# Inner RMS norms of a macaron layer: 1/rms spread over the partitions by fp32r hi/lo matmuls, the third norm summed over features by the same matmuls

## The chip, the cores and the metric

One core of one Trainium2 chip runs the whole layer in one launch. The metric is the device time of that launch in microseconds; lower is better. The kernel before takes 864.71 us, the median of three runs (863.97 to 865.85).

## What is computed

One encoder layer on x of 512 tokens by 1024 features, all in float32:

```
x = x + 0.5 * swiglu(rms(x, g1), gate1, up1, down1)      # 1024 -> 2816 -> 1024
x = x + mixer(rms(x, g2))                                # attention heads and a pooling mixer
x = x + 0.5 * swiglu(rms(x, g3), gate2, up2, down2)
x = rms(x, g4)
rms(x, g) = x * rsqrt(mean(x * x over the 1024 features) + 1e-6) * g
```

The three inner norms (the first three `rms`) are the subject here. Each token needs one number, 1/rms, and every product that follows has to be multiplied by it at some point.

## The kernel before

x lies transposed in SBUF: eight tiles of 128 features by 512 tokens. A product in float32 is made of fp32r operands: each operand is split into a rounded part `hi` (a cast on ScalarE, ACT below) and the rest `lo` (a subtraction on VectorE, DVE below), and `mm3` (lines 176 to 178) issues three matmuls of TensorE (PE below), hi*hi, hi*lo and lo*hi, into one PSUM bank. A weight panel of 128x1024 is fetched into a `raw` tile (SP's DMA queue, line 169), cast to `whi` and reduced to `wlo` (lines 131 and 132), and then feeds 24 matmuls of 512 columns. The `hi` and `lo` panels have three buffers in one pool and one in another, so a panel's cast waits until PE is through with the panel four before it.

`Norm` holds one inner norm. `add` (lines 134, 135) splits x times the gain into the token operands `hhi`, `hlo`, without 1/rms, since a factor per token can be put in after the product. `square` (lines 283 to 287) adds up x*x over the eight feature tiles in `acc`, 128 by 512. `per_token` then sums `acc` over the partitions: four fp32 matmuls, each with a 128x128 block of `acc` stationary and one column of ones moving (line 291), give one number per token in a 128x4 layout. ACT takes the root (line 298), DVE makes 1/rms of it with one Newton step on four columns (lines 301 and 261 to 264) and multiplies it into the identity (line 304), which gives `diag`, four diagonal 128x128 blocks side by side. `spread` multiplies a matrix of ones by `diag` in one fp32 matmul of 512 columns (line 312; the trace shows it as two records) and ACT copies the bank to `rb` (line 314): 1/rms of every token, the same in all 128 partitions.

`rb` has two kinds of readers, all on DVE: eight `aside` tiles x * gain * rb (line 337), from which later Strassen-like blocks of the up projection are built (lines 343, 131 to 135), and the evacuation of the gate banks (lines 395 and 399, with SiLU on ACT at 397 and the product with `up` at 687).

Each FFN begins with four banks, `first`, that take the first two feature blocks of gate and up; four panels feed them. `norm.finish()` (which calls `per_token` and `spread`) stands ahead of the last of these panels, at high priority: the Tile scheduler puts its instructions as early as their inputs allow. In the first FFN the tiles of x arrive by DMA one after the other, so this falls into the last panel of `first`. In the second FFN all of x is there, and it falls into the first panel. There it stands beside eight transposed copies of x (PE line 1431, ACT line 1435, a DMA to `x_d` at line 1436), which save x for the end. After `first`, blocks 2 to 4 are made one after the other in banks that are reused in turn: the third panel pair's first bank is `first[0]`'s, so PE cannot begin it before DVE has read `first[0]` (line 395).

The second norm sits in the mixer stage, whose order is written by a planner: generators record the instructions of PE, ACT, DVE and POOL in the order of an estimated clock. `finish_norm` there calls `per_token` and `spread` when the third weight panel is in use; its costs in the planner are not touched by the change. This norm uses `r`, the 128x4 form, as well: the projections to q, k and v put tokens on partitions.

The queues work in order: PE, ACT and DVE each take their instructions as they stand, and one that waits holds all behind it.

Of the kernel before, what the change touches and what calls it, by code (L numbers as in the profile page):

```python
# [16 lines left out]
P = 128  # L17
D = 1024
S = 512
KD = D // P  # L20
NT = S // P
# [7 lines left out]
EPS = 1e-6  # L29
# [24 lines left out]
def layer(  # L54
# [31 lines left out]
    nc = tc.nc  # L86

    const = ctx.enter_context(tc.tile_pool(name="const", bufs=1))
# [4 lines left out]
    small = ctx.enter_context(tc.tile_pool(name="small", bufs=2))  # L93
# [7 lines left out]
    def name(what):  # L101
        n_tiles[0] += 1
        return f"{what}_{n_tiles[0]}"

    def temp(dtype=F32):
        return tpool.tile([P, S], dtype, tag="t", name=name("t"))

    def bank(tag="mm", bufs=4):
        return ps.tile([P, S], F32, tag=tag, name=name(tag), bufs=bufs)

    def abank():
        return bank("a", 4)
# [15 lines left out]
    def split(src, hi, lo, scale=None):  # L128

        if scale is None:  # L130
            nc.scalar.copy(hi, src)  # L131
            nc.vector.tensor_tensor(lo, src, hi.bitcast(F32), op=ALU.subtract)  # L132
        else:
            nc.scalar.activation(hi, src, AF.Copy, scale=scale)
            nc.vector.scalar_tensor_tensor(
                lo, src, scale, hi.bitcast(F32), op0=ALU.mult, op1=ALU.subtract
            )
# [25 lines left out]
    def weights(src, parts=1):  # L163
        n = src.shape[-1]
        raw = raw_tile()
        hi, lo = part_tiles()
        for i in range(parts):
            part = slice(i * n // parts, (i + 1) * n // parts)
            nc.sync.dma_start(raw[:, part], src[:, part])
            split(raw[:, part], hi[:, part], lo[:, part])  # L170
        return hi, lo

    def mm3(acc, a, b, start, stop, further=False):

        more = dict(skip_group_check=True) if further else {}
        nc.tensor.matmul(acc, a[0], b[0], start=start, stop=False, **more)  # L176
        nc.tensor.matmul(acc, a[0], b[1], start=False, stop=False, **more)  # L177
        nc.tensor.matmul(acc, a[1], b[0], start=False, stop=stop, **more)  # L178

    def cut(pair, lo, n):  # L180
        if isinstance(pair[0], list):
            pair, lo = [z[lo // S] for z in pair], lo % S
        return pair[0][:, lo : lo + n], pair[1][:, lo : lo + n]
# [11 lines left out]
    ident = const.tile([P, P], F32, name="ident")  # L195
    make_identity(nc, ident)
    ones = const.tile([P, P], F32, name="ones")
    table = const.tile([P, 2], F32, name="table")
    nc.vector.memset(ones, 1.0)
    eps = table[:, 1:2]  # L200
    nc.vector.memset(eps, EPS)

    def tables(func, after):

        nc.scalar.activation(table[:, 0:1], after, func, scale=0.0)
# [49 lines left out]
    def rsqrt_of(v, root, out):  # L255

        n = v.shape[-1]
        y, a, b = (
            small.tile([P, n], F32, tag=f"rs{n}", name=name("rs"), bufs=3) for _ in range(3)
        )  # L260
        nc.vector.reciprocal(y, root)
        nc.vector.tensor_tensor(a, y, y, op=ALU.mult)
        nc.vector.scalar_tensor_tensor(b, a, -0.5, v, op0=ALU.mult, op1=ALU.mult)
        nc.vector.scalar_tensor_tensor(out, b, 1.5, y, op0=ALU.add, op1=ALU.mult)

    class Norm:
# [22 lines left out]
        def per_token(self, total, after=None):  # L289
            for t in range(NT):  # L290
                nc.tensor.matmul(
                    total[:, t : t + 1], self.acc[:, t * P : (t + 1) * P], ones[:, 0:1],
                    start=True, stop=True,
                )
            v, root, self.r = (
                small.tile([P, NT], F32, tag=what, name=name(what)) for what in ("v", "root", "r")
            )
            nc.scalar.activation(root, total[:, :NT], AF.Sqrt, scale=1.0 / D, bias=eps)
            if after:
                tables(after, root[:, 0:1])  # L300
            nc.vector.tensor_scalar(v, total[:, :NT], 1.0 / D, EPS, op0=ALU.mult, op1=ALU.add)
            rsqrt_of(v, root, self.r)
            self.diag = temp()
            nc.vector.tensor_tensor(
                self.diag.rearrange("p (t c) -> p t c", t=NT),
                ident.unsqueeze(1).to_broadcast([P, NT, P]),
                self.r.unsqueeze(2).to_broadcast([P, NT, P]),
                op=ALU.mult,
            )

        def spread(self, wide):
            nc.tensor.matmul(wide, ones, self.diag, start=True, stop=True)
            self.rb = small.tile([P, S], F32, tag="rb", name=name("rb"), bufs=1)
            nc.scalar.copy(self.rb, wide)

        def finish(self):
            self.per_token(abank(), AF.Silu)
            self.spread(abank())

        def blocks(self, pool, aside):  # L320

# [61 lines left out]
    def ffn_up(norm, wA, down, loaded):  # L383
# [22 lines left out]
        for kp in range(KD // 2):  # L406
            if not loaded:
                load(2 * kp)
            w = weights(wA[kp], 1 if loaded or kp else 4)
            if not loaded:  # L410
                load(2 * kp + 1)
                norm.square(2 * kp)
                norm.square(2 * kp + 1)
            if kp == KD // 2 - 1:
                with tc.high_priority():
                    norm.finish()
            for kk in range(2):
                k = 2 * kp + kk
                for j in range(4):
                    mm3(first[j], cut(w, (kk * 4 + j) * P, P), norm.h[k], k == 0, k == KD - 1)  # L420
# [127 lines left out]
        with tc.manual_schedule(engines={E.PE, E.DVE, E.Activation, E.SP}):  # L548
            last_silu = last_place = last_sums = nothing
            for n in range(PLAIN, KF):  # L550
                f = down.order[n]
                acc, up_lo, up_hi = bank()[:, :HT], bank()[:, :HT], abank()[:, :HT]
                u, z, sg = temp(), temp(), temp()
# [228 lines left out]
    def load(k):  # L782
        nc.sync.dma_start(x[k], xT[k])
        n1.add(k, square=False)
# [19 lines left out]
    with tc.tile_pool(name="act1", bufs=1, reuse_waits="tile") as apool:  # L804
        down1.begin(apool)
        ffn_up(n1, wA1, down1, loaded=False)
        p1, p5, p6 = whole(bank), whole(bank), whole(abank)

# [9 lines left out]
        with tc.manual_schedule(engines={mybir.EngineType.SP}):  # L818
# [3 lines left out]
            y = [down1.acts[i // 2][:, i % 2].rearrange("p k c -> p (k c)") for i in range(2 * NT)]  # L822
# [42 lines left out]
    with tc.tile_pool(name="mix", bufs=1, reuse_waits="tile") as mpool:  # L865
# [146 lines left out]
        v, done, scored, turned = [None] * NT, {}, set(), set()  # L1012
# [392 lines left out]
        bias = [None] * NH  # L1405
# [18 lines left out]
    with tc.tile_pool(name="act2", bufs=1, reuse_waits="tile") as apool:  # L1424
        down2.begin(apool)

        for half in range(2):
            for t in range(NT):
# [5 lines left out]
                z = temp()  # L1434
                nc.scalar.copy(z, tp)
                nc.sync.dma_start(x_d[half * NT + t], z)
        ffn_up(n3, wA2, down2, loaded=True)
        xt = [hpool.tile([P, S], F32, tag="h", name=name("xt")) for _ in range(2 * NT)]
        rooms.extend((xpool, f"x{i}", 1, 2 * S) for i in range(KD // 2))
# [28 lines left out]
        def mean(t, parts):  # L1468

            v = eps  # L1470
            for part in parts:
                u = column("u")
                nc.vector.scalar_tensor_tensor(
                    u, ssq[:, t, part : part + 1], 1.0 / D, v, op0=ALU.mult, op1=ALU.add
                )
                v = u
            return v
# [79 lines left out]
        with tc.manual_schedule(engines={E.PE, E.DVE, E.Activation}):  # L1557
            for tt in range(2):
                t = 2 + tt
                for i, at in enumerate(p7[tt]):  # L1560
                    for g, a, w in late:
                        down2.mms([[at]] * 2, g, a, w, (tt,), further=True)
                    residual(0, t, *at, scale=-0.5)
                    if i == 0 and tt:
                        settle(0, t, 0, *at[1:])
                        finish(t - 1, mean(t - 1, [1]), 0)
                        v = mean(t, [1, 0])
                    else:
                        settle(0, t, 2 * i, *at[1:])
            finish(t, v, 2)  # L1570
# [81 lines left out]
```

## Time and profile before

| what | us |
|---|---|
| median of three runs | 864.71 (863.97 to 865.85) |
| profiled execution, its own time | 865.0 |
| its span in the trace | 863.2 |
| PE busy | 848.8 |
| DVE busy | 708.3 |
| ACT busy | 501.1 |
| mean granted TensorE clock | 0.998 |

The span is what the trace covers from the first to the last instruction; the profiled execution's own time is 1.8 us longer. Both stand beside the median without a correction: 865.0 is 0.3 above 864.71. Start times in all lines are microseconds from the start of the span. In a timeline a row has start, duration, engine, line, operation and tiles, with the idle time ahead of it and what ended that in square brackets. Matmuls overlap: a matmul of 512 columns is shown with about 0.39 us but the next one starts some 0.23 us later. What a matmul costs in a full queue is the distance from start to start.

### The profile page before, as it was taken

How to read it: one execution, taken by the hardware profiler on the slowest of the kernel's cores; microseconds unless marked ns; L12 is line 12 of the kernel's file. 1: busy time of each engine (PE TensorE's matmuls, PEld its weight loads, DVE VectorE, ACT ScalarE, POOL GpSimd, SP SyncE). 2: the span in 40 equal slices, each digit the busy share in tenths (PEclk: the TensorE clock that was granted, in tenths of full speed). 3: DMA queues.
4: the chain of work that ended last, by engine and by line, in shares of the span. 5: the costliest groups of instructions: out<-in, count | busy, mean ns of one | idle time of the engine just before them, and what ended most of it. 6: DMA issues, size and time to landing. Idle time of an engine off the chain costs nothing.

```text
span 863.2 us, 14110 instructions
## 1 busy us (share of the span) xinstructions
PE 848.8 (98%) x5296; PEld 757.5 (88%) x5296; DVE 708.3 (82%) x1115; ACT 501.1 (58%) x859; POOL 120.1 (14%) x196
## 2 busy tenths in 40 slices
PE   9999999999999999989999999999999999999996
PEld 7889999999988888867878788889999999988885
DVE  7999898898897769685878667969888898887896
ACT  7445555555676556548647756445555555566573
POOL 0124322222000000120011000102112111122000
PEclk9999999999999999999999999999999999999999
DMA  8199998877576764322212026248778778899832
GB/s 291 57 285 248 293 277 207 202 206 165 144 242 204 254 212 136 97 86 85 75 57 90 25 73 244 80 140 228 212 231 202 189 199 209 251 328 341 274 109 98
DMA packets 72244, 158.50 MB, mean 184 GB/s; under 512 B 6112, under 2 KB 29168, under 8 KB 71792
## 3 DMA queue, kind: packets, MB, share of 16 engines
q1 hardware_dynamic: 49088, 110.93, 36.8%
q0 software_dynamic: 22656, 46.14, 24.7%
q8 instruction: 41, 0.67, 0.3%
q10 hardware_dynamic: 432, 0.54, 0.2%
q14 instruction: 27, 0.22, 0.1%
HBM read 153.38 MB, written 50.34 MB: 236 GB/s over the span
## 4 chain that ended last, share of the span: by engine, by line
PE 91%; DVE 3%; DMA 2%; ACT 2%; issue 1%; SPq 0%; ACTq 0%; DVEq 0%
PE mm L176 22%; PE mm L177 21%; PE mm L178 21%; PE a L176 7%; PE a L177 7%; PE a L178 7%; DMA raw<-in_wA_dram 2%; PE a L1172 1%; PE a L1226 1%; PE a L1214 1%; DVE t L1093 1%; DVE wlo L449 1%; ACT prob L1153 1%; PE a L211 0%; PE a L1431 0%
## 5 line engine op out<-in xcount | busy, mean ns | idle before, releaser
L132 DVE TENSOR_TENSOR wlo<-raw,whi 128x1024 fp32r<-128x1024 f32 (+2 forms) x115 | 125.0, 1096 | 20.7 <-ACT whi L131 20.4
L131 ACT CAST whi<-raw 128x1024 fp32r<-128x1024 f32 (+2 forms) x115 | 106.9, 944 | 57.7 <-PE mm L177 15.5
L177 PE MATMUL mm<-ha,whi 128*128 128x256 f32 x408 | 115.6, 283 | 0.0
L178 PE MATMUL mm<-ha,wlo 128*128 128x256 f32 x408 | 115.0, 282 | 0.0
L176 PE MATMUL mm<-ha,whi 128*128 128x256 f32 x408 | 115.0, 282 | 0.0
L540 ACT ACTIVATE t<-mm 128x256 f32<-128x256 f32 x102 | 39.2, 384 | 121.5 <-PE mm L178 120.8
L449 DVE TENSOR_TENSOR wlo<-wsum,whi 128x1024 fp32r<-128x1024 f32 x68 | 83.0, 1220 | 14.1 <-ACT whi L444 14.1
L178 PEld LDWEIGHTS mm<-ha,wlo 128*128 128x128 f32 x408 | 77.4, 190 | 0.0
L176 PEld LDWEIGHTS mm<-ha,whi 128*128 128x128 f32 x408 | 77.2, 189 | 0.1
L177 PEld LDWEIGHTS mm<-ha,whi 128*128 128x128 f32 x408 | 77.2, 189 | 0.1
L176 PE MATMUL mm<-hhi,whi 128*128 128x512 f32 x192 | 76.0, 399 | 0.0
L177 PE MATMUL mm<-hlo,whi 128*128 128x512 f32 x192 | 75.7, 395 | 0.0
L178 PE MATMUL mm<-hhi,wlo 128*128 128x512 f32 x192 | 74.8, 392 | 0.0
L677 POOL DMA_DIRECT2D wsum<-in_wB_dram x72 | 70.4, 1147 | 11.7 <-issue 8.5
L444 ACT CAST whi<-wsum 128x1024 fp32r<-128x1024 f32 x68 | 67.9, 1048 | 4.1 <-PE mm L177 3.9
L177 PE MATMUL mm<-wlo,ah 128*128 128x512 f32 x176 | 68.6, 390 | 0.0
L178 PE MATMUL mm<-whi,ah 128*128 128x512 f32 x176 | 68.5, 389 | 0.0
L176 PE MATMUL mm<-whi,ah 128*128 128x512 f32 x176 | 68.4, 390 | 0.0
L675 POOL COPY mark<-t 128x1 f32<-128x1 f32 x40 | 15.1, 377 | 382.1 <-DVE t L585 228.0
L449 DVE TENSOR_TENSOR wlo<-raw,whi 128x512 fp32r<-128x512 f32 x68 | 62.5, 951 | 3.4 <-ACT whi L444 3.4
L444 ACT CAST whi<-raw 128x512 fp32r<-128x512 f32 x68 | 56.3, 828 | 11.4 <-DMA raw<-in_wA_dram 6.9
L132 DVE TENSOR_TENSOR ah<-acts,ah 128x512 fp32r<-128x512 f32 (+1 forms) x72 | 45.7, 641 | 14.5 <-ACT ah L131 14.2
(211 smaller groups left out, 2381.5 us busy)
## 6 DMA issues: line engine op xcount, KB each, us to landing
raw<-in_wA_dram SPq DMA_DIRECT2D x87, 512.0 KB, 5.5
wsum<-in_wB_dram POOLq DMA_DIRECT2D x60, 512.0 KB, 7.7
raw<-wsum SPq DMA_DIRECT2D x40, 512.0 KB, 4.4
raw<-in_wB_dram SPq DMA_DIRECT2D x30, 512.0 KB, 4.7
wsum<-wsum POOLq DMA_DIRECT2D x20, 512.0 KB, 5.8
x<-in_xT_dram SPq DMA_DIRECT2D x16, 256.0 KB, 5.7
raw<-in_wQK_dram SPq DMA_DIRECT2D x8, 512.0 KB, 3.5
raw<-in_wO_dram SPq DMA_DIRECT2D x8, 512.0 KB, 3.4
```

What stands on the lines that cost most here:

```text
L131: nc.scalar.copy(hi, src)
L132: nc.vector.tensor_tensor(lo, src, hi.bitcast(F32), op=ALU.subtract)
L176: nc.tensor.matmul(acc, a[0], b[0], start=start, stop=False, **more)
L177: nc.tensor.matmul(acc, a[0], b[1], start=False, stop=False, **more)
L178: nc.tensor.matmul(acc, a[1], b[0], start=False, stop=stop, **more)
L444: nc.scalar.copy(hi, src)
L449: nc.vector.tensor_tensor(lo, src, hi.bitcast(F32), op=ALU.subtract)
L540: nc.scalar.activation(dst, src, AF.Copy, scale=scale)
L675: nc.gpsimd.tensor_copy(mark, after[:, 0:1])
L677: nc.gpsimd.dma_start(self.rows(i, g), self.rows(self.terms[i][at], g), **(dict(accum_op=ALU.add) if at else {}),)
L1093: nc.vector.tensor_tensor(q3, q3, rs[:, t, :].unsqueeze(2).to_broadcast([P, 8, HD]), op=ALU.mult)
L1153: nc.scalar.activation(p, p, AF.Copy, scale=rt)
```

## The change

All three norms: 1/rms is split into `r_hi` (fp32r) and `r_lo` on four columns, two diagonals of fp32r are made, and `spread` is two fp32r matmuls with a matrix of ones in fp32r (`ones_r`, a new tile that is cast once at the start).

The third norm (`after` is None): `acc` itself is split into a fp32r pair, and the two matmuls with `ones_r` sum it over the features and put the sum into all 128 partitions at once. There is no 128x4 form any more: root, reciprocal and Newton step run on 512 columns, and the last of these instructions writes `rb`.

```diff
+    ones_r = const.tile([P, P], F32R, name="ones_r")
     nc.vector.memset(ones, 1.0)
+    nc.vector.tensor_copy(ones_r, ones)
...
             rsqrt_of(v, root, self.r)
-            self.diag = temp()
-            nc.vector.tensor_tensor(diag, ident, self.r, op=ALU.mult)
+            r_hi = small.tile([P, NT], F32R, tag="r_hi", name=name("r_hi"))
+            r_lo = small.tile([P, NT], F32, tag="r_lo", name=name("r_lo"))
+            nc.vector.tensor_copy(r_hi, self.r)
+            nc.vector.tensor_tensor(r_lo, self.r, r_hi.bitcast(F32), op=ALU.subtract)
+            self.diag = [temp(F32R), temp(F32R)]
+            for z, r in zip(self.diag, (r_hi.bitcast(F32), r_lo)):
+                nc.vector.tensor_tensor(z, ident, r, op=ALU.mult)
+        def over_rows(self, wide, pair):
+            for i, z in enumerate(pair):
+                nc.tensor.matmul(wide, ones_r, z, start=i == 0, stop=i == 1)
         def spread(self, wide):
-            nc.tensor.matmul(wide, ones, self.diag, start=True, stop=True)
-            self.rb = small.tile([P, S], F32, tag="rb", name=name("rb"), bufs=1)
+            self.over_rows(wide, self.diag)
+            self.rb = self.broadcast()
             nc.scalar.copy(self.rb, wide)
-        def finish(self):
-            self.per_token(abank(), AF.Silu)
-            self.spread(abank())
+        def finish(self, after=None):
+            if after is not None:
+                self.per_token(abank(), after)
+                self.spread(abank())
+                return
+            pair, total = (temp(F32R), temp(F32R)), abank()
+            split(self.acc, *pair)
+            self.over_rows(total, pair)
+            root, v, y = temp(), temp(), temp()
+            nc.scalar.activation(root, total, AF.Sqrt, scale=1.0 / D, bias=eps)
+            tables(AF.Silu, root[:, 0:1])
+            nc.vector.tensor_scalar(v, total, 1.0 / D, EPS, op0=ALU.mult, op1=ALU.add)
+            nc.vector.reciprocal(y, root)
+            nc.vector.tensor_tensor(root, y, y, op=ALU.mult)
+            nc.vector.scalar_tensor_tensor(v, root, -0.5, v, op0=ALU.mult, op1=ALU.mult)
+            self.rb = self.broadcast()
+            nc.vector.scalar_tensor_tensor(self.rb, v, 1.5, y, op0=ALU.add, op1=ALU.mult)
...
-                    norm.finish()
+                    norm.finish(None if loaded else AF.Silu)
```

(The views of `diag` and of its operands are written short here.) Line numbers behind the change are larger: 291 becomes 293, 304 becomes 311, 312 becomes 320, 337 becomes 366, 395 becomes 424, 1435 becomes 1464; tile numbers differ as well.

Where the instructions stand. First norm, PE, in the last panel of `first`. Before, the one fp32 matmul with the diagonal `t_353`:

```order
L176 MATMUL mm_166<-hhi_314,whi_319 128x512
L312 MATMUL a_355<-t_353,ones 128x512
L177 MATMUL mm_166<-hlo_315,whi_319 128x512
L178 MATMUL mm_166<-hhi_314,wlo_320 128x512
L176 MATMUL mm_163<-hhi_325,whi_319 128x512
```

Of the change, the same place; `t_359` and `t_360` are the two diagonals:

```order
L177 MATMUL mm_168<-hlo_317,whi_321 128x512
L320 MATMUL a_363<-t_359,ones_r 128x512
L178 MATMUL mm_168<-hhi_316,wlo_322 128x512
L176 MATMUL mm_165<-hhi_327,whi_321 128x512
L320 MATMUL a_363<-t_360,ones_r 128x512
L177 MATMUL mm_165<-hlo_328,whi_321 128x512
```

The first of the two stands one matmul later than the old one, the second four matmuls later.

On DVE the first norm's rows of the change behind 1/rms (`r_344`) are these, in place of one row L304:

```order
L307 CAST r_hi_355<-r_344 128x4
L308 TENSOR_TENSOR r_lo_356<-r_344,r_hi_355 128x4
L311 TENSOR_TENSOR t_359<-ident,r_hi_355 128x512
L311 TENSOR_TENSOR t_360<-ident,r_lo_356 128x512
L132 TENSOR_TENSOR wlo_517<-raw_515,whi_516 128x1024
```

Before, one `aside` (L337) stood between that `wlo` and the first evacuation (L395); now the evacuation comes straight behind the `wlo`.

Third norm, PE, in the first panel of the second FFN. `a_5962` and `a_5978` are the last of the eight transposed blocks. Before:

```order
L1431 MATMUL a_5962<-ident,x_3046 128x128
L291 MATMUL a_6070<-ones,acc_5763 128x1 x4
L1431 MATMUL a_5962<-ident,x_3046 128x128
L176 MATMUL mm_5972<-hhi_5759,whi_5975 128x512
L177 MATMUL mm_5972<-hlo_5760,whi_5975 128x512
```

Of the change, from the last transposes to the first matmul with `ones_r`:

```order
L1460 MATMUL a_5978<-ident,x_3055 128x128 x2
L176 MATMUL mm_5988<-hhi_5775,whi_5991 128x512
L177 MATMUL mm_5988<-hlo_5776,whi_5991 128x512
L178 MATMUL mm_5988<-hhi_5775,wlo_5992 128x512
L176 MATMUL mm_5989<-hhi_5775,whi_5991 128x512
L177 MATMUL mm_5989<-hlo_5776,whi_5991 128x512
L178 MATMUL mm_5989<-hhi_5775,wlo_5992 128x512
L176 MATMUL mm_5986<-hhi_5795,whi_5991 128x512
L177 MATMUL mm_5986<-hlo_5796,whi_5991 128x512
L320 MATMUL a_6088<-t_6086,ones_r 128x512
```

The four matmuls with `acc` are gone. The first L320 stands eight matmuls behind the transposes, the second (of `t_6087`, the rest of `acc`) two more matmuls of the panel later; before, L312 stood thirteen matmuls behind the transposes.

ACT at the same place, of the change, from the last copy of x on. `t_6086` is the fp32r part of `acc`, the root is `t_6093`:

```order
L1464 COPY t_5983<-a_5978 128x512
L131 CAST t_6086<-acc_5779 128x512
L131 CAST whi_6021<-raw_6020 128x1024
L131 CAST whi_6051<-raw_6050 128x1024
L340 ACTIVATE t_6093<-a_6088,table 128x512
L131 CAST whi_6081<-raw_6080 128x1024
L207 ACT_TABLE_LOAD
L207 ACTIVATE table<-t_6093 128x1
L131 CAST whi_6146<-raw_6145 128x1024
L131 CAST whi_6181<-raw_6180 128x1024
```

Before, the root of four columns and the table load stood between the sixth and the eighth copy, ahead of all weight casts; now all eight copies come first, and two weight casts stand ahead of the root.

DVE at the same place, of the change, from the split of `acc` to the first evacuation:

```order
L132 TENSOR_TENSOR t_6087<-acc_5779,t_6086 128x512
L132 TENSOR_TENSOR wlo_6022<-raw_6020,whi_6021 128x1024
L132 TENSOR_TENSOR wlo_6052<-raw_6050,whi_6051 128x1024
L342 TENSOR_SCALAR t_6094<-a_6088 128x512
L343 RECIPROCAL t_6095<-t_6093 128x512
L132 TENSOR_TENSOR wlo_6082<-raw_6080,whi_6081 128x1024
L344 TENSOR_TENSOR t_6093<-t_6095 128x512
L132 TENSOR_TENSOR wlo_6147<-raw_6145,whi_6146 128x1024
L345 SCALAR_TENSOR_TENSOR t_6094<-t_6093,t_6094 128x512
L132 TENSOR_TENSOR wlo_6182<-raw_6180,whi_6181 128x1024
L347 SCALAR_TENSOR_TENSOR rb_6102<-t_6094,t_6095 128x512
```

Behind these stand the eight `aside` rows (L366) and then the first evacuation (L424). Before, six small rows (L301 to L304) came first, and the eight `aside` rows stood between the `wlo` rows; three wide rows on `aside` (L343) that stood ahead of the first evacuation now stand behind it. The second norm (mixer) has two L320 rows in the place of L312 and the same two added DVE rows as the first.

More of the change, by code (lines that the diff above doesn't have):

```diff
@@ L302, in per_token @@
             rsqrt_of(v, root, self.r)
-            self.diag = temp()
[L304 to L309, printed above, removed]
+            r_hi = small.tile([P, NT], F32R, tag="r_hi", name=name("r_hi"))
+            r_lo = small.tile([P, NT], F32, tag="r_lo", name=name("r_lo"))
+            nc.vector.tensor_copy(r_hi, self.r)
@@ new lines, in per_token @@
+            nc.vector.tensor_tensor(r_lo, self.r, r_hi.bitcast(F32), op=ALU.subtract)
+            self.diag = [temp(F32R), temp(F32R)]
+            for z, r in zip(self.diag, (r_hi.bitcast(F32), r_lo)):
+                nc.vector.tensor_tensor(
+                    z.rearrange("p (t c) -> p t c", t=NT),
+                    ident.unsqueeze(1).to_broadcast([P, NT, P]),
+                    r.unsqueeze(2).to_broadcast([P, NT, P]),
+                    op=ALU.mult,
+                )
+        def over_rows(self, wide, pair):
+            for i, z in enumerate(pair):
+                nc.tensor.matmul(wide, ones_r, z, start=i == 0, stop=i == 1)
@@ L311, in spread, with broadcast @@
+        def broadcast(self):
+            return small.tile([P, S], F32, tag="rb", name=name("rb"), bufs=1)
         def spread(self, wide):
-            nc.tensor.matmul(wide, ones, self.diag, start=True, stop=True)
-            self.rb = small.tile([P, S], F32, tag="rb", name=name("rb"), bufs=1)
+            self.over_rows(wide, self.diag)
+            self.rb = self.broadcast()
             nc.scalar.copy(self.rb, wide)
-        def finish(self):
-            self.per_token(abank(), AF.Silu)
-            self.spread(abank())
+        def finish(self, after=None):
[15 more added lines that the diff above has]
+            nc.vector.scalar_tensor_tensor(self.rb, v, 1.5, y, op0=ALU.add, op1=ALU.mult)
```

## The prediction, made before the changed kernel was run

> **What bounds the kernel now.** First the shares of the chain of waits, from the page: which engine, followed back from the last instruction, set the end.
>
> ```profile
> PE 91%; DVE 3%; DMA 2%; ACT 2%; issue 1%; SPq 0%; ACTq 0%; DVEq 0%
> ```
>
> TensorE sets it. Then the busy time of the engines in four stretches (columns: PE, PEld, DVE, ACT, POOL, clock, DMA share, GB/s): the first FFN's first Strassen blocks, the mixer, the second FFN's start, its down projection.
>
> ```profile
> 50.00:110.00 60.00, 58.94 (x445) 56.39 (x444) 53.52 (x76) 32.46 (x57) 20.36 (x26) 1.00 1.03 276
> 370.00:515.00 145.00, 140.59 (x725) 111.79 (x724) 108.57 (x258) 92.60 (x193) 14.89 (x21) 1.00 0.19 68
> 532.00:560.00 28.00, 28.00 (x125) 23.18 (x125) 27.93 (x35) 11.06 (x13) 3.26 (x3) 1.00 0.37 131
> 620.00:760.00 140.00, 140.00 (x1139) 138.20 (x1138) 121.76 (x171) 81.42 (x144) 24.76 (x42) 1.00 0.79 218
> ```
>
> PE does not pause behind the third norm (532 to 760), at full clock, so a pass less there ends the kernel earlier; but DVE is full from 532 to 560 as well, so work moved to DVE there needs care. The first stretch has full DMA queues, the second a few PE gaps. Last the chain in order of time, at the norms:
>
> ```profile
> 25.85 0.86 PE a L312 x2
> ...
> 75.86 10.56 DMA raw<-in_wA_dram
> ...
> 96.74 10.18 DMA raw<-in_wA_dram
> ...
> 360.24 0.86 PE a L312 x2
> ...
> 525.03 0.90 PE a L291 x8
> ...
> 528.86 0.23 PE mm L176
> 529.09 0.86 PE a L312 x2
> ```
>
> All three spreads and the third norm's sum are on the chain: 0.86 us each for the fp32 matmul of 512 columns, 0.90 us for the four fp32 matmuls with `acc`. A fp32r matmul of 512 columns takes 0.23 us of it.
>
> **The change part by part.** Durations for what follows, by line and shape (busy us, mean ns):
>
> ```profile
> L261 DVE RECIPROCAL rs<-root 128x4 f32<-128x4 f32 x3 | 0.5, 165 | 0.0
> L261 DVE RECIPROCAL rs<-root 128x1 f32<-128x1 f32 x4 | 0.6, 161 | 0.6 <-ACT root L1483 0.6
> L262 DVE TENSOR_TENSOR rs<-rs 128x4 f32<-128x4 f32 x3 | 0.5, 163 | 0.1
> L132 DVE TENSOR_TENSOR ha<-aside,ha 128x512 fp32r<-128x512 f32 x16 | 11.0, 687 | 4.2 <-ACT ha L131 2.7 <-PE mm L177 1.3
> L395 DVE TENSOR_TENSOR t<-mm,rb 128x512 f32<-128x512 f32 x10 | 6.8, 684 | 1.8 <-PE mm L178 1.8
> L132 DVE TENSOR_TENSOR wlo<-raw,whi 128x1024 fp32r<-128x1024 f32 x89 | 108.0, 1219 | 20.0 <-ACT whi L131 20.0
> L131 ACT CAST ha<-aside 128x512 fp32r<-128x512 f32 x16 | 10.0, 622 | 10.0 <-PE mm L177 10.0
> L131 ACT CAST whi<-raw 128x1024 fp32r<-128x1024 f32 x89 | 92.4, 1049 | 55.0 <-PE mm L177 15.5 <-PE mm L178 12.4 <-PE a L178 11.3
> L1043 ACT ACTIVATE t<-mm,r 128x512 f32<-128x512 f32 x8 | 5.5, 686 | 1.3 <-PE mm L178 1.2
> L205 ACT ACT_TABLE_LOAD x6 | 7.7, 1283 | 1.3 <-PEq L1637 1.2
> ```
>
> *Spread, three times.* One fp32 matmul (0.86) becomes two fp32r ones. No row shows fp32r with a matrix of ones, but every L176 to L178 matmul is fp32r of this shape at 0.23; the dearest neighbour is half of L312, 0.43, with which nothing is gained. I take 0.23: two make 0.46, **0.40 us less on PE in each norm**. The Trainium skill ("TensorE: Matmul & The Clock Gate", Back-to-back issue gap) gives some 131 ns per matmul of 512 columns in a sustained stream; by that the three spreads would gain 1.8 us, not 1.2, an estimate. The trace does not agree, its distance is 0.23.
>
> *First norm.* DVE gains two small rows (0.16 each) and a second diagonal (0.69), some 1.0 us, ahead of the second L320, which holds PE's queue if it is late.
>
> ```profile
> 24.48 0.69 DVE L304 TENSOR_TENSOR t<-ident,r 128x512 f32<-128x512 f32 x1
> 25.46 0.39 PE L176 MATMUL mm<-hhi,whi 128*128 128x512 f32 x1
> 25.99 1.22 DVE L132 TENSOR_TENSOR wlo<-raw,whi 128x1024 fp32r<-128x1024 f32 x1 [0.82 <-ACT whi L131]
> 27.36 0.75 DVE L337 SCALAR_TENSOR_TENSOR aside<-x,gain_sb,rb 128x512 f32<-128x512 f32 x1 [0.15 <-ACT rb L314]
> 28.03 0.68 DVE L395 TENSOR_TENSOR t<-mm,rb 128x512 f32<-128x512 f32 x1
> 61.64 0.69 DVE L132 TENSOR_TENSOR ha<-aside,ha 128x512 fp32r<-128x512 f32 x1 [0.67 <-PE mm L177]
> ```
>
> The diagonals are done at about 25.5 and 26.2. PE is at the L176 ahead of the spread at 25.46, five matmuls of 0.23 from the second L320: 26.6, so 0.4 us to spare. Most of DVE's extra 1.0 us lies in its idle 0.82 and 0.15; it comes out about 0.3 us late and meets PE again at 61.64, where it had waited 0.67 for PE. PE's lead then goes through the two fetches of 10 us. They start when DVE frees a buffer, behind PE, so they should start 0.4 earlier; with the DMA share at 1.03 they may land as late as before. Between 0 and 0.40 I take **0.30**.
>
> *Second norm.*
>
> ```profile
> 357.34 0.69 DVE L304 TENSOR_TENSOR t<-ident,r 128x512 f32<-128x512 f32 x1
> 360.72 1.23 DVE L966 TENSOR_TENSOR wlo<-raw,whi 128x1024 fp32r<-128x1024 f32 x1 [2.69 <-ACT whi L964]
> ```
>
> The diagonals are done by 359.1, a microsecond ahead of PE (360.24), and DVE sits idle for 2.69 behind them: free. **0.40** is left, unless the mixer's gaps eat it.
>
> *Third norm.* PE loses the 0.90 of L291 and gains 0.40 from the spread. What replaces them is a chain through ACT and DVE:
>
> ```profile
> 522.33 2.99 ACT L1435 COPY t<-a 128x512 f32<-128x512 f32 x6
> 522.73 0.69 DVE L287 TENSOR_TENSOR acc<-acc,t 128x512 f32<-128x512 f32 x1
> 525.86 0.48 PE L176 MATMUL mm<-hhi,whi 128*128 128x512 f32 x1
> 526.27 0.16 DVE L301 TENSOR_SCALAR v<-a 128x4 f32<-128x4 f32 x1 [2.85 <-ACT root L298]
> 529.68 2.36 DVE L132 TENSOR_TENSOR wlo<-raw,whi 128x1024 fp32r<-128x1024 f32 x2 [1.85 <-ACT whi L131]
> 534.89 2.73 DVE L337 SCALAR_TENSOR_TENSOR aside<-x,gain_sb,rb 128x512 f32<-128x512 f32 x4
> 536.34 1.06 ACT L131 CAST whi<-raw 128x1024 fp32r<-128x1024 f32 x1 [3.37 <-PE mm L177]
> 545.45 0.68 DVE L395 TENSOR_TENSOR t<-mm,rb 128x512 f32<-128x512 f32 x1
> ```
>
> `acc` is ready at 523.4, but its cast stands behind all eight copies: six end at 525.3, two more of 0.5 at 526.3, the cast (0.62) at 526.9, the subtraction (0.69) at 527.6. PE, without L291, is behind the transposes at 524.96 and eight matmuls later, at 526.8, at the first L320; it waits 0.1 there and hardly at the second (527.6). I take **0.15 lost**.
>
> Then ACT: two weight casts to 529.0, the root (0.69, as L1043 from PSUM) to 529.7, a cast to 530.75, table load and its activation to 532.2, a cast to 533.3. The fifth cast needs the buffer of PE's second panel, which runs from 529.65 (twenty matmuls behind 524.96, plus 0.15) for 24 matmuls to 535.1: cast done at 536.15. DVE, in its new order: `wlo` 529.2 and 530.4, v 531.1, reciprocal 531.8, `wlo` 533.0, square 533.7, `wlo` 534.9, 535.6, the fifth `wlo` (behind the cast) 537.4, `rb` 538.15, eight `aside`, 0.68 apart, 543.6. `first[0]` is finished 63 matmuls behind 529.65, at 543.95, so the evacuation waits for PE and is done by 544.8; PE wants the bank at 546.0. DVE gains 2.7 us of work (six rows of about 0.7 for five of 0.16 and one of 0.69), hidden in its 4.7 idle microseconds, and **1.7 us** are left before PE waits: 0.5 ahead of the evacuation, 1.2 ahead of the bank.
>
> This hangs on the reciprocal of 512 columns, which no row shows. Its rows so far (shortest, median, longest in ns):
>
> ```profile
> L261 DVE RECIPROCAL rs<-root x7: 157/164/168, 23.6 to 857.9; 128x1 f32<-128x1 f32 x4, 128x4 f32<-128x4 f32 x3
> ```
>
> From one to four columns the mean grows by 4 ns, about one per column as for the product beside it, so I take 0.7 as for L304. If all of the 11 ns between shortest and longest were for three columns, 512 would take 2.0, and the 1.3 more are still held by the 1.7. At half of 0.7 nothing would be gained, since DVE then waits longer for the fifth cast.
>
> *Sum.* 0.30 + 0.40 + 0.90 + 0.40 - 0.15 = **1.85 us**. The profiled execution takes 865.0, 0.3 above the median: 863.15 for it, and 864.71 - 1.85 = **862.9** for the median. The `ones_r` cast falls into DVE's idle start.
>
> **The rivals.** *The full DMA and the mixer take the two small gains.* For it: the share of 1.03, and 4.4 us of gaps in the mixer. Against it: the chain reaches both fetches from PE. Then 1.15 is left: 863.6.
>
> *A slow reciprocal.* A column costs DVE 1.04 ns (1219 less 687 over 512). Were each eight passes long, 512 would take some 4.4 us. The third `wlo` would be done at 536.7, while PE wants it two matmuls behind 535.1, at 535.55: PE waits 1.15; the rest lies in the waits for the fifth cast and for `first[0]`. Gain 0.7: 864.0. Four columns would then take about 25 ns more than one, not 4. The Trainium skill ("VectorE: DVE Perf Modes", First, the fixed hardware budget) has the reciprocal as an iterative divide with a repeat count of 8; the small rows do not show eight passes per element.
>
> *The 512-column chain makes DVE late (slower).* Place: the evacuation of `first[0]`. If none of the 2.7 us found an idle gap, the evacuation would end at 546.1 + 2.7 = 548.8, PE would wait 2.8, and 865.7 results; with the slow reciprocal too, 869.4. It decides from 1.7 us of lateness on, and is slower than before from 3.55. For it: DVE's 27.93 of 28. Against it: idle 2.85 and 1.85 just ahead, and three wide `aside` rows that now stand behind the evacuation.
>
> *The change doesn't do what it says:* with ones at 0.43 per pass, only L291's 0.90 - 0.15 goes: 864.0.
>
> **How the numbers follow.** Forecast 0.62 (862.3 to 863.5), small gains lost 0.17, slow reciprocal 0.08, DVE late 0.10, passes not cheaper 0.03. Leaving out DVE late and a rest, 862.1 to 864.7. A measurement of this kernel tells about 0.2%, 1.73 us, from no change: the edge is 862.98, just above my value. Some 0.40 of the forecast's 0.62 lie below it: faster 0.40. Slower by that much needs DVE late by over 5.3 us, or what I have not seen: 0.07. Same 0.53.
>
> **What would show it.** Two L320 in the chain at 0.23 each; L291 gone from the third norm; the reciprocal's row at 0.7 or far above; PE without a wait at the second FFN's third panel pair and at most 0.2 at L320; the fetch that landed at 86.4 landing at about 86. A PE wait for DVE near 546, or one for `acc`'s pair near 527 of over 0.5, would make me wrong.

## The result, and the profile after

| | before | changed |
|---|---|---|
| median, us | 865.06 (863.97 to 866.78, 22 runs) | 863.75 (862.22 to 866.23, 22 runs) |
| ratio | | 0.9983, interval 0.9976 to 0.9989 |
| profiled execution, its own time | 865.0 | 864.34 |
| span | 863.2 | 862.5 |
| PE, DVE busy | 848.8, 708.3 | 846.9, 715.1 |

1.3 us faster, 0.9 to 2.1 by the interval: 863.2 on the footing of the 864.71 that the prediction started from. 862.9 was forecast.

The shares of the chain of waits in the page of the changed kernel: PE has less, DMA 6% for 2%.

```profile
PE 86%; DMA 6%; DVE 4%; ACT 2%; issue 1%; SPq 1%; ACTq 0%; DVEq 0%
```

To see where time went, I cut the span at marks that both kernels have. The chain of waits in order of time has five of them (start, length, what), here of before: the first norm's sums, the transposes ahead of the second norm, the last products of the mixer's heads, the transposes that save x, the last instruction.

```profile
22.25 0.95 PE a L291 x8
...
342.53 1.31 PE a L836 x12
...
495.54 1.27 PE a L1226 x8
...
519.96 1.76 PE a L1431 x16
...
858.64 0.75 DVE o L1491
```

The timeline of DVE and ACT has the others: one weight sum of a Strassen step four times (line 474, behind the change 503), and the ACT table's change at the start of the first down projection.

```profile
69.50 0.69 DVE L474 TENSOR_TENSOR wsum<-wsum,raw 128x512 f32<-128x512 f32 x1
...
140.60 0.69 DVE L474 TENSOR_TENSOR wsum<-wsum,raw 128x512 f32<-128x512 f32 x1
...
255.64 0.20 ACT L205 ACTIVATE table<-ah 128x1 f32<-128x1 f32 x1
...
587.02 0.69 DVE L474 TENSOR_TENSOR wsum<-wsum,raw 128x512 f32<-128x512 f32 x1
...
736.37 0.69 DVE L474 TENSOR_TENSOR wsum<-wsum,raw 128x512 f32<-128x512 f32 x1
```

The same marks in the changed kernel, with four rows more of its chain: the second norm's spread, the third norm's two matmuls, and a load at 742 us.

```profile
22.14 0.98 PE a L293 x8
...
342.60 1.31 PE a L865 x12
...
360.33 0.46 PE a L320 x2
...
495.26 1.28 PE a L1255 x8
...
520.24 1.75 PE a L1460 x16
...
527.26 0.36 PE a L320
...
528.09 0.26 PE a L320
...
741.95 11.01 DMA raw<-in_wB_dram
...
857.93 0.75 DVE o L1520
```

```profile
69.28 0.69 DVE L503 TENSOR_TENSOR wsum<-wsum,raw 128x512 f32<-128x512 f32 x1
...
140.90 0.69 DVE L503 TENSOR_TENSOR wsum<-wsum,raw 128x512 f32<-128x512 f32 x1
...
255.18 0.20 ACT L207 ACTIVATE table<-ah 128x1 f32<-128x1 f32 x1
...
586.43 0.69 DVE L503 TENSOR_TENSOR wsum<-wsum,raw 128x512 f32<-128x512 f32 x1
...
734.40 0.69 DVE L503 TENSOR_TENSOR wsum<-wsum,raw 128x512 f32<-128x512 f32 x1
```

The stretches between these marks, in us (the first begins at the end of the sums, so 69.50 - 22.25 - 0.95 for before). The last two columns are two experiments below: each has one of the two things that the change turns out to do. A cell is one execution, but the profiles of the other experiments repeat stretches 3 to 7 within about 0.1 wherever code and tile places are the same, with one exception named below; stretches 2 and 9 they do not repeat.

| stretch, with its end before | before | changed | before + 128 bytes | changed + 384 bytes |
|---|---|---|---|---|
| 1 first norm, plain blocks, 69.5 | 46.30 | 46.16 | 46.60 | 45.93 |
| 2 Strassen blocks under full DMA, 140.6 | 71.10 | 71.62 | 71.74 | 71.77 |
| 3 more Strassen blocks, 255.6 | 115.04 | 114.28 | 114.29 | 115.03 |
| 4 first down projection, 342.5 | 86.89 | 87.42 | 87.39 | 86.86 |
| 5 second norm, mixer, 495.5 | 153.01 | 152.66 | 153.09 | 152.66 |
| 6 end of the mixer, 520.0 | 24.42 | 24.98 | 25.07 | 24.42 |
| 7 third norm, plain blocks, 587.0 | 67.06 | 66.19 | 67.39 | 65.88 |
| 8 Strassen blocks, 736.4 | 149.35 | 147.97 | 148.44 | 149.34 |
| 9 second down projection, end | 122.27 | 123.53 | 122.93 | 123.05 |

The changed kernel gains where there is a norm (5, 7), but also in 3 and 8, where nothing was changed, and loses in 2, 4, 6 and 9, where nothing was changed either. The prediction has neither.

### The profile page after: what moved, and what is told of

It reads as the page before. It is cut to its first block, busy times and chain, and to the rows that moved or that the text cites. A ratio compares the mean times of both kernels' runs of the same rounds, so it can differ in the third digit from the quotient of the medians.

```text
span 862.5 us, 14105 instructions
## 1 busy us (share of the span) xinstructions
PE 846.9 (98%) x5288; PEld 753.1 (87%) x5288; DVE 715.1 (83%) x1122; ACT 501.4 (58%) x859; POOL 120.5 (14%) x196
## 4 chain that ended last, share of the span: by engine, by line
PE 86%; DMA 6%; DVE 4%; ACT 2%; issue 1%; SPq 1%; ACTq 0%; DVEq 0%
PE mm L176 20%; PE mm L178 20%; PE mm L177 20%; PE a L176 7%; PE a L178 7%; PE a L177 7%; DMA raw<-in_wA_dram 4%; DMA raw<-in_wB_dram 1%; PE a L1201 1%; DVE wlo L478 1%; PE a L1255 1%; PE a L1243 1%; ACT whi L473 1%; DVE t L1122 1%; ACT prob L1182 1%
## 5 line engine op out<-in xcount | busy, mean ns | idle before, releaser
L704 POOL COPY mark<-t 128x1 f32<-128x1 f32 x40 | 17.0, 425 | 379.3 <-DVE t L614 225.0
```

The costliest lines, as they stand in the source:

```text
L704: nc.gpsimd.tensor_copy(mark, after[:, 0:1])
```

## The experiments

Ratios are to runs of the kernel before beside them on the same chip.

**The two halves of the change.** One kernel leaves the third norm's sums as they were:

```diff
-                    norm.finish(None if loaded else AF.Silu)
+                    norm.finish(AF.Silu)
```

> The changed spread in all three norms, but the third norm sums and takes its root as before (four fp32 matmuls with acc, 128x4 root and reciprocal). Theory: 0.40 us of PE per norm reaches the end except for some 0.1 to 0.4 in the first FFN and the mixer, so 0.8 to 1.2 us below the kernel before (863.9 to 864.3 beside 865.1), and no 3.3 us reciprocal. Rival (what PE saves ahead of the third norm is lost in DMA waits and mixer gaps): 0.4 us below, from the third norm's spread alone.

The other has the third norm's new form, and one fp32 diagonal and `ones` in the two others:

```diff
-            self.over_rows(wide, self.diag)
+            nc.tensor.matmul(wide, ones, self.diag, start=True, stop=True)
```

> The first two norms as before (one fp32 matmul with the diagonal), the third as in the change. Theory: PE loses 0.90 and 0.40 and waits 0.5 at the matmuls with ones_r, as the trace of the change shows: 0.8 us below the kernel before. Rival (the 3.34 us reciprocal holds PE up somewhere behind the third norm): no gain, or slower.

Measured: 864.25, ratio 0.9987 (0.9978 to 0.9996), and 864.74, ratio 0.9991 (0.9981 to 1.0002). By the medians the first half gives 0.3 to 1.9 us, and the second anything from 1.6 us faster to 0.2 slower. The stretches of their profiles say more. In the first kernel the tiles lie as in the changed one, so it is compared with before + 128 bytes: stretches 1, 5 and 7 take 46.20, 152.70 and 67.02, which is 0.40, 0.39 and 0.37 shorter, one spread in each. In the second they lie as before but for a move of all by 512 bytes: stretch 7 takes 65.94, 1.12 shorter than before, and stretches 1 and 3 to 6 are those of before within 0.03.

**The reciprocal.** In the first kernel a copy of the root takes its place.

```diff
-            nc.vector.reciprocal(y, root)
+            nc.vector.tensor_copy(y, root)
```

> The change with the 512-column reciprocal of the third norm replaced by a copy of 512 columns, so the output is not the layer's: it leaves out the 3.34 us. Theory (hidden by DVE's room ahead of the evacuation of the first bank): the same as the change within 0.3 us. Rival (the slow reciprocal costs PE time): faster than the change by 0.7 us or more, the price that the prediction gave it.

The second has the line twice, which changes nothing but DVE's time.

> The change with the third norm's 512-column reciprocal issued twice: 3.3 us more in DVE's queue. Theory (one reciprocal used up nearly all of DVE's room): PE waits in the third weight panel of the second FFN, since the third wlo, done at 535.3 in the change, is now done at 538.7 while PE wants it at about 535.5 to 536; 2.5 to 3.3 us slower than the change, 866.5 to 867.5 beside a kernel before of 865.3. Rival (DVE still has room, 0.5 ahead of the evacuation and 1.2 ahead of the bank): within 0.5 us of the change.

Measured: 863.55, ratio 0.9977 (0.9968 to 0.9986), and 863.30, ratio 0.9979 (0.9971 to 0.9988). Without it, with it, and with two, the time is the same within what these runs tell. My expectation of 2.5 to 3.3 us for the second one fell. The timeline of DVE in the changed kernel shows why, from the reciprocal to the evacuation of `first[0]` (line 424):

```profile
530.92 3.34 DVE L343 RECIPROCAL t<-t 128x512 f32<-128x512 f32 x1
...
539.45 5.39 DVE L366 SCALAR_TENSOR_TENSOR aside<-x,gain_sb,rb 128x512 f32<-128x512 f32 x8
544.76 0.68 DVE L424 TENSOR_TENSOR t<-mm,rb 128x512 f32<-128x512 f32 x1
```

and the kernel with two:

```profile
529.75 3.34 DVE L343 RECIPROCAL t<-t 128x512 f32<-128x512 f32 x1
533.01 1.16 DVE L132 TENSOR_TENSOR wlo<-raw,whi 128x1024 fp32r<-128x1024 f32 x1
534.09 3.34 DVE L344 RECIPROCAL t<-t 128x512 f32<-128x512 f32 x1
...
...
542.66 0.75 DVE L367 SCALAR_TENSOR_TENSOR aside<-x,gain_sb,rb 128x512 f32<-128x512 f32 x1
543.44 0.69 DVE L425 TENSOR_TENSOR t<-mm,rb 128x512 f32<-128x512 f32 x1
```

Eight `aside` products, 5.39 us, stand ahead of the evacuation in the one, and a single one in the other. With 3.3 us more on its chain the scheduler puts seven of them behind the evacuation, which comes no later: 24.4 us behind the transposes that save x, and 24.5 in the changed kernel. The third `wlo`, at which I expected PE to wait, stands ahead of the second reciprocal. PE is busy 28.00 of 28 us from 532 to 560 in both.

**The wait at the third norm's first matmul.** The cast of `acc` is taken off ACT, where it stands behind the copies of x:

```diff
-            split(self.acc, *pair)
+            nc.vector.tensor_copy(pair[0], self.acc)
+            nc.vector.tensor_tensor(pair[1], self.acc, pair[0].bitcast(F32), op=ALU.subtract)
```

> The change with the third norm's acc split on DVE alone (fp32r copy and subtraction), where DVE sits idle for 3.4 us, and not with a cast on ACT behind the eight copies of x. Theory: the pair is ready by 525 and PE's waits of 0.3 and 0.2 us at the two matmuls with ones_r go, 0.5 us faster than the change. Rival (an earlier PE only meets DVE at the first evacuation, which is late by the reciprocal): the same as the change, with a wait of about 0.5 at the third panel pair's first bank.

Measured: 863.61, ratio 0.9981 (0.9971 to 0.9990). PE's idle times at line 320 are gone (they were 0.3 and 0.2), and the time is level with the changed kernel's; the 0.5 us expected isn't there. In the chain the two rows were only 0.13 and 0.03 longer than the 0.23 of every other, and stretch 7 is 0.11 shorter than the changed kernel's.

**What a PE lead is worth at each norm.** Three kernels of before leave 16 of a panel's 24 matmuls out (a product without its hi*lo and lo*hi parts), near one norm each, 3.6 us of PE.

```diff
-                    mm3(first[j], cut(w, (kk * 4 + j) * P, P), norm.h[k], k == 0, k == KD - 1)
+                    (mm3 if loaded or kp < 3 else mm1)(first[j], ...)      # norm 1
```

> The kernel before with 16 of the 24 matmuls left out in the last panel of the first FFN's first four banks (only hi*hi is kept there, so the products are less exact): 3.6 us less of PE right behind the first norm, nothing else changed. It asks how much of a lead there reaches the end. Theory (the two late fetches start behind PE and take it over in part): 1.8 to 3.6 us faster than before. Rival (the DMA queues, full from 50 to 110, set the time there): under 1 us faster, with PE's waits for the fetched raw tiles longer by about 3.

> The kernel before with 16 of the 24 matmuls left out in the fourth weight panel of the mixer, right behind the second norm's spread (only hi*hi is kept): 3.6 us less of PE there. Theory (the gaps of the mixer start behind PE, so the lead goes through): 2.5 to 3.6 us faster. Rival (ACT and DVE set the mixer's pace, so PE waits longer in its gaps): under 1.5 us faster.

> The kernel before with 16 of the 24 matmuls left out in one bank of the second FFN's third panel pair, at 547 to 552, behind the third norm's evacuation (only hi*hi is kept): 3.6 us less of PE there. Theory (PE does not pause from 532 to 760): 3.2 to 3.6 us faster. Rival (DVE, full from 532 to 560, or the fetches take it): under 2 us faster.

Measured: 865.75, ratio 1.0004 (0.9994 to 1.0014); 863.88, ratio 0.9987 (0.9978 to 0.9995); 861.36, ratio 0.9962 (0.9949 to 0.9974). At the third norm nearly all arrives (2.2 to 4.4 us). The other two fall short of what I expected, and they do not show what I meant them to show, for PE's clock fell. Two windows, of the second kernel and of one that is described at the end of this section (columns as in the prediction's first table, the clock third from the right):

```profile
487.00:490.30 3.30, 3.30 (x13) 2.81 (x13) 2.08 (x4) 0.94 (x3) 0.00 (x0) 0.50 0.02 5
```

```profile
488.50:491.80 3.30, 3.30 (x13) 2.81 (x12) 2.02 (x4) 0.88 (x3) 0.00 (x0) 0.50 0.00 0
```

The second kernel's lead on before was 1.8 us at 484 and 0.2 at 495. In the first kernel PE waits 2.7 us for the first evacuation and then has a clock of 0.50 from 29.1 to 32.4 us. The mean clock of a run shows how often this comes: 0.996 or less in 8 of 12 runs of the first kernel and in 9 of 11 of the second, but in 1 of 22 of the changed kernel. In the other kernel of the two windows nothing was left out of the mixer, so the fall there is not owed to missing matmuls alone; they made it frequent. These two experiments say little on 0.4 us.

**The place of the tiles.** `r_hi` and `r_lo` are 128x4 each, in a pool with two buffers. They fill 16 bytes per partition; I count 32 for each of the four buffers, 128 in all, which no view shows and the runs below bear out. Every tile that is allocated behind that pool (activations, some weight buffers, the mixer's tiles) moves by 128 bytes against the weights and tokens ahead of it; `ones_r` moves all by 512. The kernel before already has a tile that is never used, at the head of that pool. I made it longer, in the kernel before by 128 bytes, with no other edit:

```diff
-    small.tile([P, 16], F32, name="step", bufs=1)
+    small.tile([P, 48], F32, name="step", bufs=1)
```

> The kernel before with one tile of its small pool 128 bytes longer; nothing is computed otherwise. In the changed kernel the two new tiles r_hi and r_lo (two buffers of 32 bytes each) moved every tile that is allocated behind the small pool by 128 bytes against the rest, and its PE pace differs from before far away from the norms: 0.2285 us from one 512-column matmul to the next in the first down projection (before 0.2266), 0.232 at 500 to 520 us (before 0.2266), and between 580 and 740 us it runs 1.5 us faster. Theory (place of the tiles): this kernel shows those paces too, without any change of the norms: about 0.7 us lost between 240 and 340, 0.45 lost between 495 and 519, some 1 us gained between 130 and 230 and some 1.5 us gained between 580 and 740, of which 1.4 is given back behind it; in all between 864.5 and 866.0. Rival (the new instructions or PE's place in its instruction stream set the pace): paces of 0.2266 as before, every lead against before constant apart from the stretch of the full DMA, time as before.

and in the changed kernel by 384 (`[P, 112]`), which makes the whole shift 1024 bytes.

> The changed kernel with 384 bytes more in the small pool, so that with the 640 that it had moved the tiles by, they all stand at the same place modulo 512 as before. Theory (place of the tiles): PE's paces are those of before (0.2266 in the first down projection and at 500 to 520); the lead gained at the second norm, 0.37, then lasts to the third, which adds 1.1; 863.2 to 864.2 in all, where the changed kernel is level with it because its faster stretches pay for its slower ones. Rival (instructions): paces as in the changed kernel, 0.2285 and 0.232.

Measured: 865.59, ratio 0.9999 (0.9988 to 1.0009), and 864.26, ratio 0.9988 (0.9975 to 1.0001). The marks of before with 128 bytes more, chain and then timeline:

```profile
22.28 0.98 PE a L291 x8
...
343.28 1.31 PE a L836 x12
...
496.37 1.27 PE a L1226 x8
...
521.44 1.76 PE a L1431 x16
...
860.20 0.75 DVE o L1491
```

```profile
69.86 0.69 DVE L474 TENSOR_TENSOR wsum<-wsum,raw 128x512 f32<-128x512 f32 x1
...
141.60 0.69 DVE L474 TENSOR_TENSOR wsum<-wsum,raw 128x512 f32<-128x512 f32 x1
...
255.89 0.20 ACT L205 ACTIVATE table<-ah 128x1 f32<-128x1 f32 x1
...
588.83 0.69 DVE L474 TENSOR_TENSOR wsum<-wsum,raw 128x512 f32<-128x512 f32 x1
...
737.27 0.69 DVE L474 TENSOR_TENSOR wsum<-wsum,raw 128x512 f32<-128x512 f32 x1
```

and those of the changed kernel with 384:

```profile
22.56 0.87 PE a L293 x8
...
343.02 1.31 PE a L865 x12
...
495.68 1.27 PE a L1255 x8
...
520.10 1.76 PE a L1460 x16
...
858.37 0.75 DVE o L1520
```

```profile
69.36 0.69 DVE L503 TENSOR_TENSOR wsum<-wsum,raw 128x512 f32<-128x512 f32 x1
...
141.13 0.69 DVE L503 TENSOR_TENSOR wsum<-wsum,raw 128x512 f32<-128x512 f32 x1
...
256.16 0.20 ACT L207 ACTIVATE table<-ah 128x1 f32<-128x1 f32 x1
...
585.98 0.69 DVE L503 TENSOR_TENSOR wsum<-wsum,raw 128x512 f32<-128x512 f32 x1
...
735.32 0.69 DVE L503 TENSOR_TENSOR wsum<-wsum,raw 128x512 f32<-128x512 f32 x1
```

Read the table of stretches by columns: 128 bytes alone make stretches 3, 4 and 6 those of the changed kernel, within 0.1 us (8 goes the same way, 0.9 of 1.4; the rest of it is open), and with 384 bytes more they and 8 are those of before, within 0.03. The theory holds; the rival (new instructions) falls. PE's distance from matmul to matmul shows it too: 0.2266 us in the first down projection (mean of 88 rows) with the tiles as before, 0.2285 with 128 bytes; from 500 to 520 us 0.2266 and 0.2315 to 0.2333. In the time all of it is worth about nothing (0.9999), since the faster stretches pay for the slower.

**One of the effects without the others.** In the Strassen stage a weight part has 1024 of 1152 columns of its buffer and starts where a list says, in floats, four sets in turn; the fourth lies in the moved pool. With the change it stands, modulo 512 bytes, where 160 bytes into its buffer would put it without. I took the changed kernel with 384 bytes more, and set all four, then the fourth alone, to 160:

```diff
-ROOM, STEPS = 1024 + 128, (16, 32, 64, 8)
+ROOM, STEPS = 1024 + 128, (40, 40, 40, 40)        # steps_160
+ROOM, STEPS = 1024 + 128, (16, 32, 64, 40)        # one_step_160
```

> The kernel with 384 bytes more, and in the Strassen stage all weight parts placed 160 bytes into their buffers instead of 64, 128, 256 and 32. In the changed kernel one set of four, moved by 128 bytes, stood 160 bytes past the tokens' place modulo 512, and its products went at 0.114 us per 256-column matmul, the other three at 0.119. Theory (the distance between the two operands modulo 512 decides): all products go at 0.114; about 1000 and 1100 matmuls in the two stretches where PE does not wait for DMA, three in four of them 4 to 5 ns faster: 6 us less, 856 to 860, unless DVE, busy 122 of 140 there, takes its place. Rival (only the buffer's own region counts, or another wait follows): 863 to 866.

> As the changed kernel with 384 bytes more, but in the Strassen stage the fourth set of weight parts (the one in the activations' pool) stands 160 bytes into its buffer instead of 32; modulo 512 it then stands where the changed kernel has it, and nothing else is moved. Theory (the place of this set alone makes the two faster products, 0.114 us per matmul instead of 0.118): the lead grows by some 0.9 from 130 to 230 us and by some 1.3 from 580 to 740, while the first down projection keeps 0.2266; 1.0 to 2.0 less than with 384 bytes alone, if the load that lands at 753 does not take the second part back; 862.3 to 863.8. Rival (the place of the token operands, which the changed kernel moved as well, makes it): paces and time as with 384 bytes alone, 864.3.

Measured for all four: 866.62, ratio 1.0013 (1.0004 to 1.0023), slower than before and outside both expectations: the rule that I had made of it, that the distance of the two operands decides, falls. Stretch 3 takes 116.10 and all products 0.120 us per matmul. For the fourth set alone: **861.45** (859.66 to 864.19, 6 runs), ratio **0.9952 (0.9936 to 0.9967)**. Its marks in the timeline:

```profile
141.66 0.69 DVE L503 TENSOR_TENSOR wsum<-wsum,raw 128x512 f32<-128x512 f32 x1
...
255.66 0.20 ACT L207 ACTIVATE table<-ah 128x1 f32<-128x1 f32 x1
...
587.12 0.69 DVE L503 TENSOR_TENSOR wsum<-wsum,raw 128x512 f32<-128x512 f32 x1
...
735.00 0.69 DVE L503 TENSOR_TENSOR wsum<-wsum,raw 128x512 f32<-128x512 f32 x1
```

Stretch 3 is 114.00, stretch 8 is 147.88: 1.0 and 1.5 us less than with 384 bytes alone, where 128 bytes gave 0.75 and 0.9, and without the losses in 4 and 6 (its distances there are 0.2266 again). The median lies 0.85 below the range that I expected. The profiled execution is the slowest of the six, 864.19: the clock of 0.50 in the second of the two windows above is from it, and makes its stretch 5 1.6 longer (154.24). The kernel beats both others, and its interval does not touch the changed kernel's. The place of that one set makes the gain; why it does stays open.

## Why the prediction was right, step by step

With the tiles in equal places, the last column of the table against before, each step can be read by itself.

- **The spread, 0.40 for each norm.** Two rows of 0.23 (0.46 in the chain) for one of 0.86: right. Stretch 5, with the second norm, is 0.35 shorter (forecast 0.40), so the mixer's gaps eat next to nothing of it. With the spread alone it was 0.40, 0.39 and 0.37 at the three norms.
- **The first norm, 0.30.** By 69.5 us stretch 1 is 0.37 shorter. What the full DMA leaves of it stays open: stretch 2 takes 70.06 to 71.99 us in the kernels measured (72.60 in the one with matmuls left out at the first norm), and 70.21 in one of them that is the kernel before up to there (71.10), so 0.4 can't be seen in it. The fetch that was to land at about 86 landed at 85.6; at 140.6, by the marks, the changed kernel has no lead.
- **The third norm, 1.15.** Stretch 7 is 1.18 shorter. PE saves 0.90 + 0.86 - 0.46 = 1.30, which leaves 0.12 for the waits ahead of the two matmuls (their rows in the changed kernel have 0.36 and 0.26 instead of 0.23); forecast was 0.15. With the third norm alone stretch 7 was 1.12 shorter.
- **Sum.** 0.37 + 0.35 + 1.18 = 1.90, forecast 1.85.

Wrong were three things, which did not show in the time or paid for each other:

- **The reciprocal, "0.7 as for L304".** It took 3.34, between my value and the 4.4 of the rival. The error was to draw a slope from 4 ns between one column and four and to carry it to 512. It cost nothing: by the prediction's own order 2.64 more puts the third `wlo` at 535.6, just when PE wants it (535.55), and it was done at 535.3; the evacuation ended at 545.4, 0.6 later than forecast, and PE did not wait. The margin of 1.7 us was no fixed one either: I took the eight `aside` rows to stand ahead of the evacuation whatever happens, and with two reciprocals the scheduler moved seven of them. The rival of a late DVE was priced on that same order, and did not come.
- **Nothing waits behind 560.** "PE does not pause behind the third norm (532 to 760), so a pass less there ends the kernel earlier." In the changed kernel it does pause: a load for the second down projection comes onto the chain (11.01 us to land at 752.96) and PE waits 0.62 for the panel made of it (0.45 with 384 bytes more). In the kernel before the same load takes some 10.1 us (issued at 744.04, its cast waits for it until 754.12) and PE does not wait. That the lead causes the wait is not shown, and two profiles speak against it. With the third norm alone the kernel is 1.98 us ahead of before at the mark of 736.4, as far as the changed kernel; its load, issued at 742.03, takes 10.3 us, PE does not wait, and stretch 9 takes 122.38. With all four sets at 160 the kernel is 1.2 behind there, and PE waits 0.49. So the 0.78 by which stretch 9 is longer with 384 bytes more has no shown cause; with 128 bytes alone it is 0.66 longer without any lead. The row of that load's cast with the third norm alone:

```profile
752.32 1.06 ACT L131 CAST whi<-raw 128x1024 fp32r<-128x1024 f32 x1 [1.75 <-DMA raw<-in_wB_dram]
```

- **The unchanged code keeps its pace.** The prediction took all of PE's distances outside the edits as given. 128 bytes changed them by -4% to +3%, up to 0.9 us a stretch and either way, with a sum near nothing here.

So 1.90 came out of the steps. In the profile of the changed kernel other things lie over it: the moved tiles gain 1.05 in stretches 3, 4, 6 and 8 together and lose some 0.6 in 1 and 7 (46.60 and 67.39 with 128 bytes alone, for 46.30 and 67.06), and stretches 2 and 9 add 0.5 and 1.3. The medians say 1.3 (0.9 to 2.1) for the change and 1.0 (-0.1 to 2.2) for it with the tiles in place. Both intervals hold 1.85 too, so the times alone do not show that anything of it was lost behind the steps. The right total is owed to the steps, and in part to luck: I did not see the moved tiles, which change the pace of most of the kernel and happened to sum to nearly nothing.

## What to carry to other kernels

A small new tile can move all others: when a stretch that a change doesn't touch runs faster or slower, compare PE's distance from matmul to matmul there, and shift the tiles by themselves before explaining anything else. Cut the span at marks and compare stretches; a total of 1.3 us in 865 held parts of -1.4 to +1.3. A slope between two tiny shapes says nothing of a large one. A stretch without PE gaps in one profile need not be without them in the next: ask which load comes next and how much its time to land varies.

## What the runs showed of the hardware that I had not expected

- A reciprocal of 128x512 in float32 takes 3.34 us on DVE: (3342 - 161) / 511 = 6.2 ns a column beside about 1.0 for a product, while one and four columns take 161 and 165 ns.
- The place of operands in SBUF, by 128 bytes, changes the distance of matmuls: 0.2266 to 0.2285 and 0.232 at 512 columns, and two of the Strassen products from 0.118 to 0.113 at 256 columns, the others by about +0.001 or less. The Trainium skill ("SBUF — State Buffer", SBUF: two separate sides) has PE never waiting on another engine's access, with contention only at the port pair of VectorE and GpSimd and at the AXI ports. Nothing in that makes the place of a tile matter to PE; in these runs it does, and what PE meets there is not settled.
- PE's granted clock fell to 0.50 for at least 3.3 us in three profiles: behind a hole of 2.7 us in PE's work, and twice in the mixer, where PE's longest idle time ahead of it was 1.1 us. The Trainium skill ("TensorE: Matmul & The Clock Gate", Part 1) gives half the clock after an idle window of about 3.4 us. The half agrees; the window does not, as PE had no idle time of that length in any of the three. The kernel before has the same gaps in the mixer at full clock, so what decides is open.
